# Attention norms, row broadcast and conv taps of the input projection moved to other ticks, and low parts of wide weights on one engine

## Chip, cores and metric

One Trainium2 chip, one core. The metric is the device time of one execution in microseconds; a median over runs is given.

## What is computed

One layer of a hybrid block on x of 1024 rows and 1024 columns, in float32 (depth 1):

```
h = rms_norm(x, mix_norm_g)
u = h @ w_in                       # 3328 columns, split over three mixers
q, k, v -> 4 heads of stick-breaking attention (q and k normed by head)
rq, rk, rv, rg -> 8 heads of retention in chunks, normed, times silu(rg)
a, gate -> GLU, causal depthwise conv of 31 taps, layer norm over 256 channels, silu
x = x + concat(three outputs) @ w_out
x = x + relu(rms_norm(x) @ w_ff1)^2 @ w_ff2
```

## The kernel before

**Products.** Every large product is done in three TensorE matmuls on float32 split in a high and a low part (`mm3`, L117): high by high, and the two mixed ones. For each weight chunk of 128 x 512 ScalarE copies the high part (L181, or L153 for chunks that go to a "wr" tile) and VectorE or GpSimd subtracts it to get the low part (L182, L154). Chunks come by DMA on SP's queue into five buffers, and a buffer is free for the next load when the low part is made.

**Input projection.** x is loaded with its norm's weights applied and multiplied at once by the first wide group (q and k of head pair 0, and v), L202 to L228, into all eight PSUM banks, which are then copied to SBUF (`raw0`). The row norm's factors `rstd` come at the end of that stage (`row_stats`, L243). After that the work is cut in ticks (`tick`, L269): in each, PE gets a part of a product, and before it the side work that was entered for that tick with `at_tick`, by its order number. Ticks 0 to 15: the narrow product for head pair 1 (`gemm_narrow`, 8 row tiles of 128, two ticks each, two PSUM banks "g"). Ticks 16 to 31: conv columns a and gate. Ticks 32 to 95: four wide groups of 16 ticks (`gemm_group`): k and v, then g and q of retention's first half, then the same for the second half. Ticks 96 to 111: the first half of the output projection (three of eight rows of w_out), then the rest, and the feed-forward part.

**Wide weights.** A wide group has eight chunks (`w_wide`, L141). Chunks are counted in `nwide` over all groups; 1 to 8 are the first group, 9 to 16 the second, 17 to 40 the third to fifth. An odd number has its low part on VectorE, an even one on GpSimd. Nine tiles hold them in turn, so of the eight chunks of a group all but one are split while the last row tile of the group before uses the same tiles.

**Side work.** `sb_norm` (L287) norms one row tile's q and k by head: a square on ScalarE, a sum on VectorE, a power on GpSimd (`rpow`), a product on VectorE. `sb_turn` (L301) transposes four tiles on PE and splits them. `sb_head` (L334) enters for each head 12 attention steps, one a tick: `a_step` (scores, sigmoids, scan, product), two ticks later `b_step` (transposes and split), then `c_step` (product by v). Tiles 0 to 3 of pair 0 are normed before tick 0, tiles 4 to 7 within `turn0(0)` at tick 1, and `turn0(1)` is at tick 3. `row_bcast` (L249), which spreads `rstd` over all partitions for the conv gate, is at tick 16. `qk1_evac` norms a tile of pair 1 two ticks after its product began, and frees its bank.

**Conv.** 124 taps (`conv_tap`, VectorE, L591), entered from tick 35 on by the list `per`; the late half of the rows (hf 1) first, then the early half. The layer norm of two row tiles has two parts, `conv_norm_a` and two ticks later `conv_norm_b` (L595, L616).

**Output projection.** `split_mixed` (L763) splits a 128-row part of the mixers' output; `out_proj` (L854) adds up three rows (0 to 2) for all output tiles first, then the other five (3 to 7) in the order of their numbers. The rows 6 and 7 are split after the last tick of side work.

The order on each engine's queue is not the code's order alone: when the program is built, a planner simulates the engines and takes the ready instruction that comes first in the code. Once built, each engine goes through its queue strictly in order.

Of the kernel before, what the change touches and what calls it, by code (L numbers as in the profile page):

```python
# [15 lines left out]
P = 128  # L16
# [3 lines left out]
NT = T // P  # L20
# [58 lines left out]
def build(tc, d):  # L79
# [59 lines left out]
    nwide = [0]  # L139

    def w_wide():  # L141

        c = wpos[1]
        wpos[1] += 1
        w_dma(c + RAW + (2 if c >= RAW else 0))
        n = nwide[0] % 9
        nwide[0] += 1
        lo_engine = V if nwide[0] % 2 else GP
        if n < WB:
            return w_split(raws[c], lo_engine)  # L150
        t = wp.tile([P, 1024], F32R, tag="wr", name=nm("ww"), bufs=3)
        hi, lo = t[:, 0:512], t[:, 512:1024]
        S.copy(hi, raws[c])  # L153
        lo_engine.tensor_tensor(out=lo, in0=raws[c], in1=hi.bitcast(F32), op=ALU.subtract)  # L154
        return hi, lo
# [93 lines left out]
    def row_bcast(out, col, tag, by="cv"):  # L249
        for hf in range(2):  # L250
            ps = bank(tag)
            dg = small(by, (P, 4, P))
# [34 lines left out]
    def sb_norm(pair, tt, src):  # L287
# [7 lines left out]
        if tt % 2 == 0:  # L295
            tb[tt // 2] = small("cv", (P, 2, 256))
        qn = tb[tt // 2][:, tt % 2, :]
# [3 lines left out]
    def sb_turn(pair, tg):  # L301
        pq, pk = bank("t"), bank("t")
        for u in range(4):
            qn = tb[2 * tg + u // 2][:, u % 2, :]
            TE.transpose(pq[:, u * P:u * P + P], qn[:, 0:P], ident)
            TE.transpose(pk[:, u * P:u * P + P], qn[:, P:2 * P], ident)
# [26 lines left out]

    def sb_head(pair, e, t0):  # L334
        h = 2 * pair + e
        tick0 = t0
        for m in range(4):
# [66 lines left out]
            for jg in range((2 * m + 1) // 4, -1, -1):  # L404
                for ii in range(2):
                    at_tick(t0, 30, lambda a=(m, jg, ii, None, st): a_step(*a))
                    at_tick(t0 + 2, 20, lambda a=(m, jg, ii, None, st): b_step(*a))
                    t0 += 1
                at_tick(t0 + 2, 10, lambda a=(m, jg, None, st): c_step(*a))
# [61 lines left out]
    def turn0(tg):  # L471
        sb_turn(0, tg)
        if tg == 0:
            norm0(range(4, 8))

    norm0(range(4))
    for tt in range(NT):
        v_evac(tt, raw0[tt // 2][:, tt % 2, 256:512])
    at_tick(1, 5, lambda: turn0(0))
    at_tick(3, 5, lambda: turn0(1))  # L480
    t1 = sb_head(0, 0, 2)
    t1 = sb_head(0, 1, t1)
    t1 = sb_head(1, 0, t1)
    sb_end = sb_head(1, 1, t1) + 4
# [9 lines left out]
    rbc = slot("DM")  # L494
    at_tick(now[0], 6, lambda: row_bcast(rbc, rstd, "o"))
# [137 lines left out]
    per = [1] * 22 + [2] * 7 + [3] * 16 + [2] * 20  # L633
# [4 lines left out]
    for t2, t in ((2, 81), (3, 85), (0, 100), (1, 102)):  # L638
# [215 lines left out]
    def out_proj(pi, dt, hf):  # L854
# [3 lines left out]
        for k in w:  # L858
            mm3(ps, w[k][0], w[k][1], mh[k][:, tsl], ml[k][:, tsl], k == min(w), k == max(w))
# [14 lines left out]
    for dt in range(NK):  # L874
        out_job(0, dt)
        if dt in (1, 5, 6):
            split_mixed({1: 3, 5: 4, 6: 5}[dt])
# [314 lines left out]
```

## Time and profile before

| | |
|---|---|
| median of 3 runs | 1157.6 us (1157.25 to 1157.94) |
| the profiled execution | 1159.54 us |
| its span, first to last instruction | 1157.8 us |
| mean granted TensorE clock | 0.992 |
| PE busy | 1121.4 us, 97% of the span |
| PE weight loads busy | 933.0 us, 81% |
| DVE busy | 897.7 us, 78% |
| ACT busy | 484.1 us, 42% |
| POOL busy | 519.1 us, 45% |

PE is TensorE, DVE VectorE, ACT ScalarE, POOL GpSimd, SP the DMA queue. A timeline row has its start, its duration, engine, code line, operation, output<-inputs, shapes and a count, and in brackets the idle time before it with the instruction that ended it. Matmuls overlap, so their durations are longer than the distance of their starts.

### The profile page before, as it was taken

To read this page: it belongs to the slowest core of one execution; us is meant where nothing else is said; L and a number is where in the kernel's file an instruction comes from. 1 tells how busy PE (TensorE), PEld (TensorE's weight loads), DVE (VectorE), ACT (ScalarE), POOL (GpSimd) and SP (SyncE) were. 2 spreads that over 40 slices of the span, in tenths; PEclk is the share of its full clock that TensorE was granted. 3 is DMA by queue.
4 is the path that set the end of the run, shared out by engine and by line. 5 is a ranking of instruction groups with operands and counts; after the bars stand their busy time and mean duration, and the time that the engine had idled before them with its cause. 6 is when DMAs were issued, how large, how long until landed. Compare 5 with 4: busy or idle time off the path is not lost.

```text
span 1157.8 us, 15678 instructions
## 1 busy us (share of the span) xinstructions
PE 1121.4 (97%) x5416; PEld 933.0 (81%) x5416; DVE 897.7 (78%) x1378; ACT 484.1 (42%) x917; POOL 519.1 (45%) x413
## 2 busy tenths in 40 slices
PE   8968899999999989999999999999999999999997
PEld 6857788888887878888888888888878788888886
DVE  7498677787899898579975666666699897886963
ACT  7366655453322242356433333333443443444441
POOL 4356234473555463242466565655583531522300
PEclk9989999999999989999999999999999999999999
DMA  8101011030202051112254444444787464552342
GB/s 277 48 1 46 19 42 55 19 110 15 87 24 87 20 217 61 55 73 91 78 187 148 152 161 140 164 146 141 279 304 264 130 219 129 164 182 82 110 136 73
DMA packets 63727, 137.00 MB, mean 118 GB/s; under 512 B 7200, under 2 KB 11936, under 8 KB 63648
## 3 DMA queue, kind: packets, MB, share of 16 engines
q1 hardware_dynamic: 63072, 135.56, 35.3%
q8 instruction: 43, 0.70, 0.3%
q10 hardware_dynamic: 576, 0.44, 0.1%
q14 instruction: 36, 0.29, 0.1%
HBM read 98.22 MB, written 37.75 MB: 117 GB/s over the span
## 4 chain that ended last, share of the span: by engine, by line
PE 47%; DVE 5%; issue 3%; POOL 2%; ACT 0%; DVEq 0%; POOLq 0%; ACTq 0%
PE g L119 4%; PE g L120 4%; PE g L118 4%; PE t L119 4%; PE t L118 4%; PE t L120 4%; PE o L119 4%; PE o L120 4%; PE o L118 4%; PE z L119 4%; PE z L118 4%; PE z L120 4%; DVE wlo L182 1%; POOL sum L903 1%; POOL wr L903 0%
## 5 line engine op out<-in xcount | busy, mean ns | idle before, releaser
L182 DVE TENSOR_TENSOR wlo<-sum,whi 128x512 fp32r<-128x512 f32 x78 | 80.2, 1029 | 84.2 <-ACT whi L181 84.1
L181 ACT CAST whi<-sum 128x512 fp32r<-128x512 f32 x78 | 47.9, 617 | 101.4 <-POOL sum L903 50.9
L182 DVE TENSOR_TENSOR wlo<-wr,whi 128x512 fp32r<-128x512 f32 x80 | 76.4, 960 | 6.9 <-ACT whi L181 6.9
L908 POOL TENSOR_TENSOR sum<-wr 128x512 f32<-128x512 f32 x16 | 23.4, 1466 | 120.2 <-DMA wr<-in_w_ff_dram 92.7
L365 POOL TENSOR_TENSOR be<-be,kp 128x512 f32<-128x512 f32 (+3 forms) x48 | 44.6, 932 | 70.5 <-DVE kp L361 33.1
L181 ACT CAST whi<-wr 128x512 fp32r<-128x512 f32 x80 | 48.2, 620 | 51.7 <-PE t L119 17.6
L196 POOL TENSOR_TENSOR rs<-ss,nhalf 128x4 f32<-128x4 f32 (+1 forms) x36 | 36.8, 1024 | 66.8 <-DVE ss L699 44.7
L361 DVE TENSOR_TENSOR_SCAN kp<-kp 128x512 f32<-128x512 f32 (+3 forms) x48 | 53.4, 1118 | 10.1 <-ACT kp L354 9.8
L591 DVE SCALAR_TENSOR_TENSOR DM__439_2052<-glu,vec,DM__439_2052 128x512 f32<-128x512 f32 x60 | 52.7, 921 | 0.0
L591 DVE SCALAR_TENSOR_TENSOR glu<-glu,vec 128x512 f32<-128x512 f32 x60 | 50.3, 881 | 0.0
L354 ACT ACTIVATE kp<-z 128x512 f32<-128x512 f32 (+3 forms) x48 | 23.7, 493 | 36.2 <-PE z L351 22.0
L182 POOL TENSOR_TENSOR wlo<-wraw,whi 128x512 fp32r<-128x512 f32 x18 | 28.4, 1585 | 22.6 <-ACT whi L181 21.2
L903 POOL TENSOR_TENSOR sum<-wr,sum 128x512 f32<-128x512 f32 x19 | 32.8, 1725 | 9.9 <-DVE wlo L182 9.9
L903 POOL TENSOR_TENSOR sum<-sum,wr 128x512 f32<-128x512 f32 x18 | 24.4, 1357 | 12.5 <-DVE wlo L182 12.5
L376 PE MATMUL t<-ident,be 128*128 128x128 f32 x144 | 25.1, 276 | 4.2 <-DVE P__108_534 L315 1.6
L181 ACT CAST whi<-wraw 128x512 fp32r<-128x512 f32 x33 | 20.1, 619 | 19.5 <-PE g L119 10.0
L563 POOL TENSOR_TENSOR P__538_2584<-P__397_1882 128x128 f32<-128x128 f32 x16 | 14.5, 906 | 29.0 <-DVE P__397_1882 L561 29.0
L182 POOL TENSOR_TENSOR wlo<-rawq,whi 128x512 fp32r<-128x512 f32 x14 | 23.7, 1699 | 7.8 <-ACT whi L181 7.5
L355 ACT ACTIVATE be<-z 128x512 f32<-128x512 f32 (+3 forms) x48 | 23.7, 493 | 8.4 <-PE t L376 8.4
L376 PEld LDWEIGHTS t<-ident,be 128*128 128x128 f32 x144 | 16.9, 140 | 8.1 <-issue 5.7
L903 POOL TENSOR_TENSOR wr<-wr,wr 128x512 f32<-128x512 f32 x16 | 22.5, 1406 | 1.1
L681 ACT ACTIVATE e<-o 128x256 f32<-128x256 f32 x16 | 6.2, 385 | 38.6 <-PE o L679 37.9
(2941 smaller groups left out, 4141.6 us busy)
## 6 DMA issues: line engine op xcount, KB each, us to landing
wr<-in_w_ff_dram SPq DMA_DIRECT2D x40, 512.0 KB, 3.9
wraw<-in_w_in_dram SPq DMA_DIRECT2D x32, 256.0 KB, 2.7
rawq<-in_w_in_dram SPq DMA_DIRECT2D x20, 256.0 KB, 2.8
P__396_1881<-in_rot_dram SPq DMA_DIRECT2D x32, 128.0 KB, 2.0
wraw<-in_w_out_dram SPq DMA_DIRECT2D x10, 256.0 KB, 2.8
rawq<-in_w_out_dram SPq DMA_DIRECT2D x6, 256.0 KB, 3.5
P__18_144<-in_xT_dram SPq DMA_DIRECT2D x1, 512.0 KB, 5.1
P__24_182<-in_xT_dram SPq DMA_DIRECT2D x1, 512.0 KB, 6.2
```

Source lines behind the costliest of these rows:

```text
L118: TE.matmul(out, lh, rh, start=start, stop=False, skip_group_check=on)
L119: TE.matmul(out, lh, rl, start=False, stop=False, skip_group_check=on)
L120: TE.matmul(out, ll, rh, start=False, stop=stop, skip_group_check=on)
L181: S.copy(hi, raw)
L182: (lo_engine or GP).tensor_tensor(out=lo, in0=raw, in1=hi.bitcast(F32), op=ALU.subtract)
L196: GP.tensor_tensor(out=out, in0=in_, in1=nhalf[:, 0:in_.shape[1]], op=ALU.pow)
L354: S.activation(kp[:, 0:n], pz[:, 0:n], AF.Sigmoid, scale=-0.125)
L361: V.tensor_tensor_scan(rev, rev, rev, kp[:, n:n + 1], op0=ALU.mult, op1=ALU.bypass)
L365: GP.tensor_tensor(out=be[:, 0:n], in0=be[:, 0:n], in1=kp[:, 1:n + 1], op=ALU.mult)
L376: TE.transpose(pt[:, j * P:j * P + P], be[:, j * P:j * P + P], ident)
L591: V.scalar_tensor_tensor(out=acc, in0=src, scalar=vec[:, o:o + 1], in1=acc, op0=ALU.mult, op1=ALU.add)
L903: (eng or GP).tensor_tensor(out=o, in0=x, in1=y, op=ALU.subtract)
```

## The change

The low parts of wide chunks from number 17 on are all made on POOL. `row_bcast` is done before tick 0, with its operands in two pages instead of the "cv" buffers. All eight tiles of pair 0 are normed before tick 0, into pages of their own; their two turns are at ticks 3 and 6 instead of 1 and 3. Attention steps follow a list of ticks: ten from tick 6 on, one a tick; then 20 in ticks 16 to 30; then one a tick from 31. The taps from tick 35: one a tick for 15 ticks, two for 14, three for 16, then one and two in turn for 16, then one for 9, up to tick 104. The layer norms begin at ticks 72, 76, 105 and 107 (81, 85, 100 and 102 before). The second half of the output projection adds up the rows in the order 3, 6, 7, 4, 5, and rows 4 and 5 are both split after output tile 6 of the first half.

```diff
--- before.py
+++ after.py
@@ -145,7 +145,7 @@
         w_dma(c + RAW + (2 if c >= RAW else 0))
         n = nwide[0] % 9
         nwide[0] += 1
-        lo_engine = V if nwide[0] % 2 else GP
+        lo_engine = V if nwide[0] % 2 and nwide[0] <= 16 else GP
         if n < WB:
             return w_split(raws[c], lo_engine)
         t = wp.tile([P, 1024], F32R, tag="wr", name=nm("ww"), bufs=3)
@@ -249,7 +249,7 @@
     def row_bcast(out, col, tag, by="cv"):
         for hf in range(2):
             ps = bank(tag)
-            dg = small(by, (P, 4, P))
+            dg = small(by, (P, 4, P)) if by else page(10 + hf, (P, 4, P))
             V.tensor_tensor(out=dg, in0=ident.unsqueeze(1).to_broadcast([P, 4, P]),
                             in1=col[:, 4 * hf:4 * hf + 4].unsqueeze(2).to_broadcast([P, 4, P]), op=ALU.mult)
             TE.matmul(ps, ones, dg.rearrange("p a b -> p (a b)"), start=True, stop=True)
@@ -293,15 +293,18 @@
         rs = small("rs", (P, 4))
         rpow(rs, ss)
         if tt % 2 == 0:
-            tb[tt // 2] = small("cv", (P, 2, 256))
-        qn = tb[tt // 2][:, tt % 2, :]
+            if pair == 0:
+                tb[0, tt // 2] = nrm0[tt // 4][:, tt % 4:tt % 4 + 2, :]
+            else:
+                tb[1, tt // 2] = small("cv", (P, 2, 256))
+        qn = tb[pair, tt // 2][:, tt % 2, :]
         V.tensor_tensor(out=qn.rearrange("p (a b) -> p a b", b=DH), in0=src.rearrange("p (a b) -> p a b", b=DH),
                         in1=rs.unsqueeze(2).to_broadcast([P, 4, DH]), op=ALU.mult)
 
     def sb_turn(pair, tg):
         pq, pk = bank("t"), bank("t")
         for u in range(4):
-            qn = tb[2 * tg + u // 2][:, u % 2, :]
+            qn = tb[pair, 2 * tg + u // 2][:, u % 2, :]
             TE.transpose(pq[:, u * P:u * P + P], qn[:, 0:P], ident)
             TE.transpose(pk[:, u * P:u * P + P], qn[:, P:2 * P], ident)
         ts = slice(tg * 512, tg * 512 + 512)
@@ -331,9 +334,11 @@
 
     mix_sb = {}
 
+
+    sb_ticks = list(range(6, 16)) + [16 + 3 * (i // 4) + (0, 0, 1, 2)[i % 4] for i in range(20)] + list(range(31, 60))
+
     def sb_head(pair, e, t0):
         h = 2 * pair + e
-        tick0 = t0
         for m in range(4):
             st = {"carry": {}, "first": True}
 
@@ -403,10 +408,10 @@
 
             for jg in range((2 * m + 1) // 4, -1, -1):
                 for ii in range(2):
-                    at_tick(t0, 30, lambda a=(m, jg, ii, None, st): a_step(*a))
-                    at_tick(t0 + 2, 20, lambda a=(m, jg, ii, None, st): b_step(*a))
+                    at_tick(sb_ticks[t0], 30, lambda a=(m, jg, ii, None, st): a_step(*a))
+                    at_tick(sb_ticks[t0] + 2, 20, lambda a=(m, jg, ii, None, st): b_step(*a))
                     t0 += 1
-                at_tick(t0 + 2, 10, lambda a=(m, jg, None, st): c_step(*a))
+                at_tick(sb_ticks[t0] + 2, 10, lambda a=(m, jg, None, st): c_step(*a))
         return t0
 
     def parts(n, lo_engine=None):
@@ -470,18 +475,19 @@
 
     def turn0(tg):
         sb_turn(0, tg)
-        if tg == 0:
-            norm0(range(4, 8))
-
-    norm0(range(4))
+
+    rbc = slot("DM")
+    row_bcast(rbc, rstd, "o", None)
+    nrm0 = [page(19, (P, 4, 256)), page(10, (P, 4, 256))]
+    norm0(range(NT))
     for tt in range(NT):
         v_evac(tt, raw0[tt // 2][:, tt % 2, 256:512])
-    at_tick(1, 5, lambda: turn0(0))
-    at_tick(3, 5, lambda: turn0(1))
-    t1 = sb_head(0, 0, 2)
+    at_tick(3, 5, lambda: turn0(0))
+    at_tick(6, 5, lambda: turn0(1))
+    t1 = sb_head(0, 0, 0)
     t1 = sb_head(0, 1, t1)
     t1 = sb_head(1, 0, t1)
-    sb_end = sb_head(1, 1, t1) + 4
+    sb_head(1, 1, t1)
     mix_sb[1] = page(17)
     sb_prepare(1)
 
@@ -491,8 +497,6 @@
             at_tick(now[0] + 1, 5, lambda: sb_turn(1, tt // 4))
 
     gemm_narrow(qk1_evac)
-    rbc = slot("DM")
-    at_tick(now[0], 6, lambda: row_bcast(rbc, rstd, "o"))
     glu = [None, None]
 
     def conv_gate(ct, hf, pa, pgt):
@@ -630,12 +634,12 @@
 
     c0 = 35
     taps = [(ct, hf, j) for hf in (1, 0) for j in range(TAPS) for ct in range(2)]
-    per = [1] * 22 + [2] * 7 + [3] * 16 + [2] * 20
+    per = [1] * 15 + [2] * 14 + [3] * 16 + [1, 2] * 8 + [1] * 9
     n, t = 0, c0
     while n < len(taps):
         at_tick(t, 40, lambda a=taps[n:n + per[t - c0]]: conv_taps(a))
         n, t = n + per[t - c0], t + 1
-    for t2, t in ((2, 81), (3, 85), (0, 100), (1, 102)):
+    for t2, t in ((2, 72), (3, 76), (0, 105), (1, 107)):
         at_tick(t, 25, lambda t2=t2: conv_norm_a(t2))
         at_tick(t + 2, 25, lambda t2=t2: conv_norm_b(t2))
 
@@ -855,8 +859,9 @@
         tsl = slice(512 * hf, 512 * hf + 512)
         w = taken[pi, dt]
         ps = bank("o" if pi else "g")
-        for k in w:
-            mm3(ps, w[k][0], w[k][1], mh[k][:, tsl], ml[k][:, tsl], k == min(w), k == max(w))
+        ks = (3, 6, 7, 4, 5) if pi else tuple(w)
+        for k in ks:
+            mm3(ps, w[k][0], w[k][1], mh[k][:, tsl], ml[k][:, tsl], k == ks[0], k == ks[-1])
         V.tensor_tensor(out=x2[dt][:, tsl], in0=ps, in1=x2[dt][:, tsl], op=ALU.add)
 
     jobs = [(pi, dt) for pi in range(2) for dt in range(NK)]
@@ -873,8 +878,11 @@
 
     for dt in range(NK):
         out_job(0, dt)
-        if dt in (1, 5, 6):
-            split_mixed({1: 3, 5: 4, 6: 5}[dt])
+        if dt == 1:
+            split_mixed(3)
+        if dt == 6:
+            split_mixed(4)
+            split_mixed(5)
     while steps:
         tick()
     for hf in range(2):
```

## Rows read from the trace of the kernel before

**Rows 1.** Windows: stretch, length, busy us of PE PEld DVE ACT POOL, PEclk, DMA, GB/s

```profile
50.00:130.00 80.00, 64.46 (x424) 55.64 (x424) 64.88 (x142) 49.99 (x107) 39.10 (x38) 0.94 0.06 17
...
300.00:390.00 90.00, 87.33 (x446) 72.80 (x445) 87.89 (x145) 24.37 (x56) 48.47 (x46) 1.00 0.21 67
390.00:400.00 10.00, 10.00 (x74) 9.29 (x73) 5.60 (x17) 3.41 (x9) 3.86 (x5) 1.00 0.00 1
...
420.00:430.00 10.00, 6.86 (x42) 5.98 (x42) 9.95 (x16) 4.41 (x11) 6.32 (x5) 0.92 0.97 366
430.00:440.00 10.00, 9.34 (x35) 7.45 (x35) 9.95 (x22) 0.75 (x2) 5.99 (x7) 0.74 0.68 263
440.00:490.00 50.00, 49.78 (x267) 41.97 (x266) 35.19 (x74) 16.68 (x37) 11.83 (x14) 1.00 0.15 45
```

**Rows 2.** Timeline of PE, 54 to 105 us: narrow product, attention, first conv matmul

```profile
54.92 0.28 PE L118 MATMUL g<-whi,xh__12_101 128*128 128x256 f32 x1
...
57.68 0.29 PE L120 MATMUL g<-whi,xl__59_380 128*128 128x256 f32 x1
...
72.23 0.41 PE L118 MATMUL g<-whi,xh__12_101 128*128 128x256 f32 x1
...
102.47 0.62 PE L376 MATMUL t<-ident,be 128*128 128x128 f32 x4
...
103.16 0.39 PE L351 MATMUL z<-P__70_448,P__69_447 128*128 128x512 f32 x1
...
104.79 0.50 PE L118 MATMUL g<-xh__12_101,whi 128*128 128x512 f32 x1 [1.11 <-DVE cv L298]
```

**Rows 3.** Timeline of DVE, 63 to 72 us: turn, scans, first evacuation

```profile
63.61 0.74 DVE L315 SCALAR_TENSOR_TENSOR P__69_447<-t,vec,P__69_447 64x512 fp32r<-64x512 f32 x1
...
70.29 1.13 DVE L361 TENSOR_TENSOR_SCAN kp<-kp 128x128 f32<-128x128 f32 x2
71.45 0.42 DVE L298 TENSOR_TENSOR cv<-g,rs 128x256 f32<-128x256 f32 x1
```

**Rows 4.** Timeline of PE at 428 us: retention's output waits for its state

```profile
428.26 0.76 PE L678 MATMUL o<-P__396_1881,P__538_2584 128*128 128x128 f32 x2 [3.13 <-DVE P__396_1881 L695]
```

**Rows 5.** Timeline of DVE and PE, 124 to 127 us: the row broadcast

```profile
124.13 0.72 DVE L253 TENSOR_TENSOR cv<-ident,rstd 128x512 f32<-128x512 f32 x1
...
124.91 1.12 PE L255 MATMUL o<-cv,ones 128*128 128x512 f32 x2 [0.59 <-DVE cv L253]
126.50 1.10 PE L255 MATMUL o<-cv,ones 128*128 128x512 f32 x2 [0.47 <-DVE kp L357]
```

**Rows 6.** Taps of line L591 (ns min/median/max); timeline of DVE and POOL at 304

```profile
L591 DVE SCALAR_TENSOR_TENSOR glu<-glu,vec x60: 710/742/1778, 343.2 to 443.8; 128x512 f32<-128x512 f32 x60
...
304.15 1.76 DVE L591 SCALAR_TENSOR_TENSOR DM__439_2052<-glu,vec,DM__439_2052 128x512 f32<-128x512 f32 x1
...
303.64 1.72 POOL L182 TENSOR_TENSOR wlo<-rawq,whi 128x512 fp32r<-128x512 f32 x1
```

**Rows 7.** Timeline of POOL and PE at the boundaries of the last three wide groups

```profile
235.44 1.94 POOL L154 TENSOR_TENSOR ww<-rawq,ww 128x512 fp32r<-128x512 f32 x1
...
243.99 1.74 POOL L182 TENSOR_TENSOR wlo<-wraw,whi 128x512 fp32r<-128x512 f32 x1
...
247.80 0.39 PE L118 MATMUL g<-whi,xh__58_379 128*128 128x512 f32 x1
...
307.22 1.71 POOL L182 TENSOR_TENSOR wlo<-wraw,whi 128x512 fp32r<-128x512 f32 x1 [1.86 <-ACT whi L181]
309.32 1.32 POOL L196 TENSOR_TENSOR rs<-ss,nhalf 128x4 f32<-128x4 f32 x1 [0.40 <-DVE ss L699]
310.63 1.27 POOL L182 TENSOR_TENSOR wlo<-rawq,whi 128x512 fp32r<-128x512 f32 x1
...
315.27 0.39 PE L118 MATMUL g<-whi,xh__58_379 128*128 128x512 f32 x1
...
365.74 1.27 POOL L182 TENSOR_TENSOR wlo<-wraw,whi 128x512 fp32r<-128x512 f32 x1 [2.26 <-ACT whi L181]
```

## Prediction, made before the changed kernel ran

> **What bounds the kernel now.** I read the windows first, because the page's slices are too coarse for waits of one to three microseconds. TensorE (PE) is the bound: from 130 us on it is nearly always busy. So the time is PE's work, plus its idle time, plus what is lost while its clock is granted at half. Two places hold nearly all that this change can reach [rows 1]. From 50 to 130 us PE is busy 64.46 of 80 us, so 15.5 us are idle, with VectorE (DVE) busy 64.88; the mean granted clock of 0.94 stands for 0.06 x 80 x 2 = 9.6 us at 1.2 GHz, of which PE worked some 6.6 us, so that about 3.3 us are lost. From 420 to 440 us PE idles 3.1 + 0.7 us, and 0.92 and 0.74 stand for 1.6 + 5.2 = 6.8 us at half clock, 3.4 us lost. Between them, from 300 to 390 us, DVE is saturated (87.89 of 90) while PE loses only 2.7 us.
>
> Then I read the two places in order of time. In the first, the last matmul of the narrow product's first two row tiles stands at 57.68 and the next one of that product at 72.23 [rows 2]. What it needs is a PSUM bank: both banks "g" are full until the first evacuation ends, and that evacuation's last DVE operation starts only at 71.45 [rows 3], because it stands in DVE's queue behind the head-pair-0 turn, of which 63.61 is the first row, and two scans at 70.29. In the second place the planner has put splits of the mixed rows ahead of retention's state update, DVE comes late to it, and PE waits 3.13 us at 428.26 [rows 4].
>
> **Part A: norms, row broadcast and turn moved at the start.** All PE work here stays; it is only placed elsewhere. The two products of the DVE row broadcast (0.72 and, alike, 0.7 us, [rows 5]) come ahead of the gate at 71.45: +1.4 us. The pair-0 turn now has tick 3 and stands behind the first evacuation (tick 2): two L315, two L318 and two L321, with 0.74 for the first [rows 3]; the six sum to 3.8 us. The scans of 1.13 us [rows 3] go to tick 6. So the gate opens at 72.23 + 1.4 - 3.8 - 1.1 = 68.7, 3.5 us earlier. What this buys is less than 3.5, since PE had used the wait for transposes and for four score steps, which now follow. From the gate to the first conv matmul at 104.79 lie 12 ticks of 1.44 us (24 matmuls from 54.92 to 57.80 are two ticks, [rows 2]) = 17.3 us; the other 15.3 us are side work and waits, and I leave them but for 0.9 us that the steps kept from the wait add. The conv product then starts 2.6 us earlier. It begins with about two more attention steps still to do: four transposes are 0.62 us and a score product 0.39 [rows 2], with the products by the values about 1.4 us a step by estimate, so +2.8 us. The row broadcast's two PE products (1.12 and 1.10) are gone from there, -2.2, and with them their waits of 0.59 and 0.47 [rows 5], -1.1. **A = -2.6 + 2.8 - 2.2 - 1.1 = -3.1 us.** The broadcast's products now lie in idle time and cost nothing; if that cover is gone they are +2.2. One wait is new: the norms of tiles 4 to 7 go into the page from which PE reads the broadcast's first product, so they, and on DVE all queued behind them, the first evacuation too, wait for PE to have read it. PE does this before DVE comes to tile 4, so 0; else one product, +1.1. The ends: +1.4 if the evacuation is planned no earlier and the broadcast only delays it; -10 if DVE, with 15.1 us unused in the 80 [rows 1], is kept busy there. I take a value near the small end, as PE is not the engine that sets this stage.
>
> The attention steps that are moved into the conv product's ticks put 20 steps into 15 ticks. DVE has room there, and PE is full anyway, so they cost what they cost before.
>
> **Part B: fewer taps late.** Ticks 80 to 95 hold 24 taps instead of 32; eight go to ticks 50 to 63 or to 96 and after, where DVE has room (35.19 of 50 us from 440 to 490, [rows 1]). Only the last half counts: from 390 to 400 DVE is idle for 4.4 us [rows 1], so no delay is carried over it. Ticks 88 to 95 lose four taps of 0.742 us [rows 6], 3.0 us, against the 3.13 us by which the state update came late [rows 4]. With it PE's wait goes to about 0.1, and the clock has no reason to fall: 3.1 + 3.4 = 6.5 us. The planner may put the splits, or other things, there again. **B = -4.5 us**, with ends 0 and -7.2 (also the 0.66 us that remain of the idle time).
>
> **Part C: the early half of the conv norm**, moved from ticks 81 and 85 to 72 and 76, and the taps of ticks 80 to 87. PE loses 2.7 us from 300 to 390; I take **-0.5 us**, with ends 0 and -2.7.
>
> **Part D: low parts on POOL alone.** Of the 24 wide chunks from the third group on, 12 low parts leave DVE. It hardly helps DVE: beside a POOL low part of 1.72 us a tap takes 1.76 instead of 0.742 [rows 6], so each moved operation takes about 1.0 us from DVE and gives back a like time. What counts is when POOL has the last low part of a group. At the first boundary POOL has no gap from 235.44 to the end of the last low part at 243.99 + 1.74 = 245.7; three more of 1.7 put that at 250.9, and PE wants it at 248.0 (its high part goes in at 247.80): 2.9 us late [rows 7]. Behind them on POOL wait the attention's products and the rotary; the transposes and the retention wait for those. The loaded chunk is freed later too, and with it the next load on SP, by no more than the low part is late. At the second boundary POOL waits 1.86 us for the high part, the last low part ends at 311.9, and three more of 1.5 to 1.7 less that gap make 315.1 at most, against 315.27. At the third it has 2.26 us of waiting [rows 7] and is taken at 0. So ends of 0 and +2.9; PE can put side work into the wait, and I take **D = +1.5 us**.
>
> **Part E: the end of the conv chain.** The last norm goes from tick 104 to 109 and the splits of rows 4 and 5 follow it; against that the second half of the output projection takes 3, 6, 7 before 4, 5. From 440 to 490 PE idles only 0.22 us [rows 1]. Two norms of five ticks later have the whole last job as cover; **+0.5 us**, with ends 0 and +2.
>
> DMA sources, sizes and their queue (SP) stay in the same order; POOL issues none. The sum: -3.1 - 4.5 - 0.5 + 1.5 + 0.5 = **-6.1 us**. The profiled execution took 1159.54 us, 1.7 over its span and 1.9 over the median 1157.6; the sum makes it 1153.4, and a median of **1151.5 us**.
>
> **The rivals.** (1) POOL becomes the bound at the boundaries, and the change is slower. For: POOL is gapless at the first one, and its low parts stretch when DVE works beside them (1.72 and 1.74 against 1.27, 1.94 at most in these rows, [rows 6, 7]). Against: at the other two it has waiting time left. At 2.2 us each the first boundary comes out 2.9 + 6 x 0.5 = 5.9 us late, the second 303.64 + 6 x 2.2 + 1.32 (a norm's power between them, [rows 7]) = 318.2 against 315.27, 2.9 late, and the third like it: 11.7 in all, -8.1 + 11.7 + 0.5 = +4.1, 1161.7 us. It decides from 7.6 us of waits in all, a mean of about 2.0 us a low part. The Trainium skill (SBUF — State Buffer, Who interferes with whom) says that VectorE with two SBUF operands and GpSimd exclude each other on a shared port pair, the later one standing still for the whole instruction. The stretched tap and low part agree with it; by that rule this rival's time would be the one to expect if each low part met a whole DVE operation. (2) Only one half of the gain comes: the planner again queues splits ahead of the state update, so B = 0: -1.6 us, 1156.0. The order on each queue is planned at compile time, which speaks for it; the shorter DVE queue speaks against. A case of this is that the moves do not move anything, as PE already ran four ticks ahead of the turn: A = 0 and B = -4.5 give 1154.6. (3) More is gained: A near -8, B near -6.5: 1144.6. DVE's unused 15.1 us speak for it; the chain DVE, POOL, DVE of each norm speaks against.
>
> **How the numbers follow.** Forecast 0.50, rival 1 0.13, rival 2 0.22, rival 3 0.15. About 0.2% (2.3 us) is what a measurement of this kernel can tell from no change. The forecast and rival 3 are faster by more, with a small part of rival 2 (1154.6): 0.67; the rest of rival 2 and a small part of the rest are within it: 0.20; slower 0.13. The range takes the forecast, most of rival 3 and rival 2: 1144.5 to 1158.5.
>
> **What would show it.** A: the gap from 57.68 to the fifth tick shrinks to some 11 us and the conv product starts near 102; wrong if the first evacuation still stands behind the turn. B: no wait of 3 us and no clock below 1 around 415 to 435. D: low parts of POOL in a row at each boundary, and PE waits on them under 3 us in all; wrong if they hold PE longer than 7 us. E: no PE wait over 2 us at the first jobs of the second half.

## The result, and the profile after

| | before | changed |
|---|---|---|
| median | 1157.77 us (1157.25 to 1159.38, 4 runs) | 1169.26 us (1166.27 to 1170.57, 4 runs) |
| ratio | | 1.0093, 95% interval 1.007 to 1.0116 |
| profiled execution, its span | 1159.54, 1157.8 us | 1170.57, 1168.8 us |
| mean granted clock | 0.992 | 0.985 |

The change costs about 1%, where 6 us less were forecast. The page of the changed kernel, its first lines and the slices of PE and of its clock:

```profile
span 1168.8 us, 15654 instructions
...
PE 1128.3 (97%) x5416; PEld 938.5 (80%) x5416; DVE 886.8 (76%) x1366; ACT 482.4 (41%) x917; POOL 540.7 (46%) x425
...
PE   8969999999999898999999999999999999999998
...
PEclk9979999999999999999999999999999999999999
```

PE has as many matmuls as before; at the lower mean clock they take 7 us longer, and PE idles 4 us more. DVE has 11 us less to do and POOL 22 more, but neither sum says where the time went. The windows do (columns as in [rows 1]):

```profile
50.00:130.00 80.00, 67.91 (x414) 58.99 (x413) 59.49 (x132) 45.27 (x93) 35.72 (x33) 0.89 0.06 17
...
360.00:370.00 10.00, 7.51 (x33) 5.04 (x33) 10.00 (x12) 4.63 (x10) 10.00 (x8) 1.00 0.35 93
370.00:380.00 10.00, 9.48 (x38) 7.49 (x36) 5.72 (x13) 1.26 (x3) 7.56 (x8) 0.83 0.49 144
380.00:390.00 10.00, 7.22 (x26) 5.62 (x27) 8.27 (x14) 2.12 (x5) 5.21 (x6) 0.83 0.09 28
430.00:440.00 10.00, 7.72 (x48) 6.21 (x46) 10.00 (x10) 7.14 (x17) 9.04 (x7) 1.00 1.00 374
440.00:450.00 10.00, 7.61 (x39) 7.05 (x40) 9.94 (x22) 0.38 (x1) 3.33 (x4) 0.83 0.81 315
...
490.00:500.00 10.00, 6.67 (x25) 4.93 (x24) 4.84 (x7) 2.98 (x5) 1.46 (x2) 0.84 0.01 2
```

Three places behind 300 us are new or no better: the third group boundary (360 to 390), where before PE lost only 2.7 us in 90 [rows 1]; the place where PE waited for retention's state update (430 to 450), as bad as before; and 490 to 500, where before there was hardly a wait. The timeline of PE there and at the start of the conv product, each with the wait ahead of it in brackets:

```profile
100.88 0.50 PE L118 MATMUL g<-xh__12_101,whi 128*128 128x512 f32 x1 [0.57 <-DVE cv L301]
...
366.14 0.50 PE L119 MATMUL g<-ww,xh__31_222 128*128 128x512 f32 x1 [0.72 <-POOL ww L154]
367.83 0.50 PE L119 MATMUL g<-wlo,xh__40_265 128*128 128x512 f32 x1 [0.72 <-POOL wlo L182]
...
381.91 0.41 PE L660 MATMUL t<-ident,P__398_1903 128*128 128x128 f32 x2 [2.43 <-DVE e L632]
...
442.39 0.98 PE L671 MATMUL z<-P__543_2611,P__544_2612 128*128 128x128 f32 x3 [3.91 <-DVE P__545_2613 L672]
...
496.08 0.73 PE L118 MATMUL o<-xh__875_4690,whi 128*128 128x512 f32 x2 [2.85 <-ACT xh__875_4690 L773]
```

The first line answers to 104.79 in [rows 2]: the conv product starts 3.9 us earlier, as part A wanted. The wait of 3.91 answers to the 3.13 of [rows 4]; PE now waits there for another retention operation on DVE, the masking of the scores (L672), where before it waited for the state.

To see where time is won or lost I set the two traces side by side by the PE work that is still to do, and took the difference of the times: the **offset**, negative where a kernel is ahead of the kernel before. For the changed kernel it is -2.9 us at 240 us, 0 at 340, +8.9 at 395, +7.5 at 480, +12.6 at 505 and some +13 at the end (its span is only 11 longer, since the stretch behind the last matmul is 2 us shorter). Where the order of PE's work differs, how the matmuls are weighed moves such a value by about 1 us. So the start wins some 3 us, the boundaries up to 340 lose 3, the third boundary with the conv norm 9, and the tail 5.

One trace's offset is not sharp. The kernel e2 below has the same PE queue as the kernel before up to some 180 us, and still its offset is +4.3 at 140 us, some 3 of them gathered between 80 and 140. Its windows show why: the granted clock is 0.83 in two slices where that of before is 1.00:

```profile
80.00:90.00 10.00, 8.59 (x55) 8.18 (x56) 7.06 (x20) 4.38 (x12) 4.76 (x6) 0.83 0.01 2
...
130.00:140.00 10.00, 8.17 (x32) 6.34 (x31) 5.54 (x12) 3.42 (x7) 0.41 (x1) 0.83 0.00 0
```

So I read rises within a stretch, and medians for the sums.

### The profile page after: what moved, and what is told of

It reads as the page before. It is cut to its first block, busy times and chain, and to the rows that moved or that the text cites. A ratio compares the mean times of both kernels' runs of the same rounds, so it can differ in the third digit from the quotient of the medians.

```text
span 1168.8 us, 15654 instructions
## 1 busy us (share of the span) xinstructions
PE 1128.3 (97%) x5416; PEld 938.5 (80%) x5416; DVE 886.8 (76%) x1366; ACT 482.4 (41%) x917; POOL 540.7 (46%) x425
## 4 chain that ended last, share of the span: by engine, by line
PE 81%; DVE 11%; issue 2%; POOL 2%; DMA 2%; ACT 1%; SPq 0%; POOLq 0%; DVEq 0%; ACTq 0%
PE g L118 11%; PE g L119 10%; PE g L120 10%; PE t L118 5%; PE t L119 5%; PE t L120 5%; PE o L119 5%; PE o L120 5%; PE o L118 5%; PE z L119 4%; PE z L118 4%; PE z L120 4%; DVE DM__444_2079 L595 2%; DVE glu L595 2%; PE o L400 1%
## 5 line engine op out<-in xcount | busy, mean ns | idle before, releaser
L182 DVE TENSOR_TENSOR wlo<-sum,whi 128x512 fp32r<-128x512 f32 x78 | 83.1, 1066 | 79.5 <-ACT whi L181 79.4
L595 DVE SCALAR_TENSOR_TENSOR glu<-glu,vec 128x512 f32<-128x512 f32 x60 | 53.0, 925 | 0.1
L182 POOL TENSOR_TENSOR wlo<-wraw,whi 128x512 fp32r<-128x512 f32 x23 | 36.3, 1590 | 16.9 <-ACT whi L181 16.9
L182 POOL TENSOR_TENSOR wlo<-rawq,whi 128x512 fp32r<-128x512 f32 x17 | 27.8, 1642 | 21.2 <-ACT whi L181 21.2
L911 POOL TENSOR_TENSOR sum<-sum,wr 128x512 f32<-128x512 f32 x18 | 25.3, 1405 | 12.6 <-DVE wlo L182 12.6
L567 POOL TENSOR_TENSOR P__543_2611<-P__403_1908 128x128 f32<-128x128 f32 x16 | 14.7, 918 | 28.5 <-DVE P__403_1908 L565 19.7
L671 PE MATMUL z<-P__543_2611,P__544_2612 128*128 128x128 f32 x128 | 18.6, 287 | 3.9 <-DVE P__545_2613 L672 3.9
L181 ACT CAST whi<-rawq 128x512 fp32r<-128x512 f32 x23 | 14.0, 618 | 18.4 <-issue 12.8
```

The source lines that it names most:

```text
L181: S.copy(hi, raw)
L182: (lo_engine or GP).tensor_tensor(out=lo, in0=raw, in1=hi.bitcast(F32), op=ALU.subtract)
L595: V.scalar_tensor_tensor(out=acc, in0=src, scalar=vec[:, o:o + 1], in1=acc, op0=ALU.mult, op1=ALU.add)
L911: (eng or GP).tensor_tensor(out=o, in0=x, in1=y, op=ALU.subtract)
```

## The experiments

| kernel | median us (runs) | ratio to before, 95% interval |
|---|---|---|
| e1_moves_only | 1167.52 (4) | 1.0057 to 1.0098 |
| e2_lo_only | 1162.49 (9) | 1.0020 to 1.0044 |
| e3_norm_later | 1160.94 (10) | 1.0005 to 1.0038 |
| e4_last_group_split | 1164.68 (4) | 1.0039 to 1.0073 |
| e5_start_only | 1154.66 (9) | 0.9943 to 0.9976 |
| e6_tail_as_before | 1162.29 (11) | 1.0015 to 1.0044 |
| e7_start_and_taps | 1155.35 (12) | 0.9968 to 1.0000 |
| e8_norm_early_only | 1167.66 (7) | 1.0045 to 1.0089 |
| e9_split_on_pool | 1156.26 (11) | 0.9967 to 0.9988 |
| e10_no_late_taps | 1151.91 (4) | 0.9935 to 0.9963 |
| e11_one_norm_early | 1158.88 (11) | 0.9989 to 1.0014 |
| e12_norm_early_fewer_taps | 1154.56 (10) | 0.9960 to 0.9981 |
| e13_start_norm_taps | 1152.01 (6) | 0.9920 to 0.9959 |
| e14_change_taps_moved | 1155.54 (12) | 0.9960 to 0.9990 |
| e15_taps_off_both | 1152.12 (7) | 0.9929 to 0.9964 |

The kernel before had medians of 1158.19 (e1 to e4), 1158.31 (e5 to e8), 1158.55 (e9 to e12) and 1158.40 (e13 to e15) beside them. "Over before" is against these.

### Which part costs: undoing one at a time (e1 to e4)

e1, against the changed kernel:

```diff
-        lo_engine = V if nwide[0] % 2 and nwide[0] <= 16 else GP
+        lo_engine = V if nwide[0] % 2 else GP
```

> All the moves of the change, but low parts of wide chunks in turn on VectorE and GpSimd as before. Theory P (the loss is GpSimd's queue at the last two group boundaries: behind the low parts there stand the conv norm's power and products, and TensorE waits): most of the 12 us come back that TensorE is late by at the end, and the time is at or below that of the kernel before, 1148 to 1157 us. Theory N (the early half of the conv norm, moved onto the boundary, and the late end of the conv chain cost it, whoever makes the low parts): 1163 to 1169 us, and TensorE still loses over 6 us from 355 to 395 us.

e2 makes the opposite edit in the kernel before.

> The kernel before with nothing but the low parts from chunk 17 on made by GpSimd. Theory P: slower than the kernel before by 3 to 9 us (1161 to 1167), with TensorE's waits at the wide groups' boundaries. Theory N: within 3 us of the kernel before (1155 to 1161), as no conv norm lies at a boundary.

e3 and e4, each against the changed kernel:

```diff
-    for t2, t in ((2, 72), (3, 76), (0, 105), (1, 107)):
+    for t2, t in ((2, 81), (3, 85), (0, 105), (1, 107)):
```

> The changed kernel with the first two conv norms back at ticks 81 and 85 (72 and 76 in the change). Theory N: the 8.6 us that TensorE loses from 355 to 395 us fall to under 3, 1161 to 1164 us. Theory P: the low parts of the last boundary still hold TensorE and the norm, 1167 to 1171 us.

```diff
-        lo_engine = V if nwide[0] % 2 and nwide[0] <= 16 else GP
+        lo_engine = V if nwide[0] % 2 and not 16 < nwide[0] <= 32 else GP
```

> The changed kernel, but in the last wide group alone (chunks 33 to 40) the odd low parts are made by VectorE again; the queues differ from the changed kernel only around that boundary. Theory P: of the 8.6 us lost from 355 to 395 us at least 5 come back, 1160 to 1165 us. Theory N: under 2 us come back, 1167 to 1170 us.

The changed kernel is 11.5 us over before. Without POOL's low parts (e1) it is still 9.3 over; with the first two conv norms back (e3) only 2.8; the low parts alone (e2) cost 4.3. So the early norm is a large term; the low parts cost less, and within the change (e1 against it) less than the two intervals can separate. e1 shows that the norm does not need them: at the third boundary its offset rises from +1.5 to +9.6, with PE waiting 2.17 and 1.53 us for low parts of DVE in place of POOL's. In e4 the time is one that theory P names, but the place is not: the rise from 360 to 400 us is 6.9 against 8.6 in the changed kernel, and the rest of its 5 us lies ahead of that place, where the clock's chance shifts are as large, so e4 tells little of the last group. In all of e1, e3 and e4 PE waits 2.85 or 2.86 us between 487 and 497 us for ACT's split of the late conv row, and the offset rises by 4 to 6 there.

### The third boundary (e8, e11, e12)

e8, against the kernel before (its taps end their late half in tick 72, so 73 is the first tick that can take a norm):

```diff
-    for t2, t in ((2, 81), (3, 85), (0, 100), (1, 102)):
+    for t2, t in ((2, 73), (3, 77), (0, 100), (1, 102)):
```

> The kernel before with only the first two conv norms moved from ticks 81 and 85 to 73 and 77 (the taps as before end their first half at 72). Theory N (the norm's chain over PE, DVE, POOL and ACT at the third group boundary costs PE by itself): the offset rises by 5 to 8 us from 350 to 400 us, waits of over 1.5 us on PE at the norm's transposes or at the retention behind them, 1163 to 1166 us. Theory P (it costs only together with low parts that POOL makes alone): under 2 us, 1158 to 1160 us.

1167.66: these eight ticks alone cost 9.4 us, nearly as much as the whole change. Theory N holds, and POOL's rule is not needed. Windows of e8, then its timeline at the boundary:

```profile
340.00:350.00 10.00, 10.00 (x49) 8.16 (x48) 10.00 (x18) 1.58 (x4) 3.78 (x4) 1.00 0.08 26
350.00:360.00 10.00, 10.00 (x50) 8.36 (x49) 10.00 (x19) 2.77 (x6) 4.27 (x5) 1.00 0.09 27
...
370.00:380.00 10.00, 8.63 (x28) 6.65 (x28) 7.39 (x14) 0.47 (x1) 4.78 (x5) 0.68 0.36 108
```

```profile
367.11 1.21 DVE L182 TENSOR_TENSOR wlo<-rawq,whi 128x512 fp32r<-128x512 f32 x1
...
370.09 1.59 DVE L182 TENSOR_TENSOR wlo<-wraw,whi 128x512 fp32r<-128x512 f32 x1
...
381.92 0.54 DVE L628 TENSOR_SCALAR e<-t,vec 128x256 f32<-128x256 f32 x1 [4.54 <-ACT e L626]
...
368.37 0.50 PE L119 MATMUL g<-wlo,xh__40_265 128*128 128x512 f32 x1 [2.17 <-DVE wlo L182]
371.74 0.80 PE L119 MATMUL g<-wlo,xh__52_341 128*128 128x512 f32 x1 [1.36 <-DVE wlo L182]
383.85 0.41 PE L656 MATMUL t<-ident,P__392_1877 128*128 128x128 f32 x2 [2.43 <-DVE e L628]
```

DVE has no gap from 340 us to the boundary. The norm's operations come on top, and so both low parts that PE needs there start late. PE waits for them, its clock falls to half (0.68 in the slice), and the transposes of the second norm come late on PE. DVE then stands 4.54 us for the sigmoid behind these, and PE 2.43 us for a "t" bank that this norm still holds: the delay goes round from one engine to the next.

e11, against the kernel before:

```diff
-    for t2, t in ((2, 81), (3, 85), (0, 100), (1, 102)):
+    for t2, t in ((2, 73), (3, 85), (0, 100), (1, 102)):
```

> The kernel before with only the first conv norm moved, from tick 81 to 73; the second stays at 85. Theory 1 (the loss of the early norms comes from the second one, whose products now stand at the third group boundary): under 2 us, 1158 to 1160 us, no PE wait of 2.43 us near 384 us. Theory 2 (each norm costs by its own work that DVE has to do before the boundary): half the loss, 1162 to 1163 us. Theory 3 (the first one carries it): 1165 us or more.

1158.88, 0.3 over before: theory 1 in time. Some waits came at the boundary (2.82 for a low part of DVE at 370.16) and were made good later. So the loss comes with the second norm. That norm moved alone was not run, so the loss may also need both.

e12 is e8 with fewer taps in ticks 73 to 80. By the list `per` they are 8 instead of 23, fifteen fewer, and not eight as the expectation below says; from tick 81 on it has three a tick, 24 in ticks 88 to 95 where before has 16:

```diff
-    per = [1] * 22 + [2] * 7 + [3] * 16 + [2] * 20
+    per = [1] * 22 + [2] * 7 + [3] * 9 + [1] * 8 + [3] * 18
```

> The kernel with the early norms alone (ticks 73 and 77), and eight taps fewer in ticks 73 to 80: one a tick there, three a tick behind them. Theory 1 (DVE is overfull ahead of the boundary, so low parts and the norm come late): the waits of 2.17 and 1.36 us on DVE's low parts go, and the offset against the kernel before rises by under 4 us instead of 8 from 350 to 400 us, 1161 to 1163 us. Theory 2 (the norm's chain over four engines with two banks and queues in fixed order makes the waits, whatever DVE's load): the 2.43 us at the transposes of the retention stay and the rise is 6 us or more, 1166 us.

1154.56: 13.1 us under e8 by moving 15 x 0.742 = 11.1 us of DVE work [rows 6] behind the boundary, and 4.0 under before. (In the traces 12 of L591's taps start from 340 to 370 us, in e8 23.) Theory 1, and more than it asked. The relief without the early norms was not run, so the 4.0 may be the relief's alone, and what the norms cost on a relieved DVE is not shown. Windows of e12, then its low parts:

```profile
340.00:350.00 10.00, 10.00 (x48) 8.16 (x48) 7.97 (x18) 1.58 (x4) 4.48 (x5) 1.00 0.09 26
350.00:360.00 10.00, 10.00 (x50) 8.32 (x49) 7.49 (x17) 3.95 (x8) 5.37 (x7) 1.00 0.10 28
360.00:370.00 10.00, 10.00 (x49) 8.27 (x48) 10.00 (x12) 3.62 (x7) 10.00 (x8) 1.00 0.57 170
```

```profile
361.58 1.22 DVE L182 TENSOR_TENSOR wlo<-rawq,whi 128x512 fp32r<-128x512 f32 x1
...
366.13 1.00 DVE L182 TENSOR_TENSOR wlo<-wraw,whi 128x512 fp32r<-128x512 f32 x1
```

DVE has 4.5 us to spare in the 20 ahead of the boundary, the low parts start 5.5 and 4.0 us earlier, and PE works through 360 to 370 without a gap.

### The tail (e6)

e6, against the changed kernel:

```diff
-    per = [1] * 15 + [2] * 14 + [3] * 16 + [1, 2] * 8 + [1] * 9
-    for t2, t in ((2, 72), (3, 76), (0, 105), (1, 107)):
+    per = [1] * 15 + [2] * 14 + [3] * 16 + [2] * 20
+    for t2, t in ((2, 72), (3, 76), (0, 100), (1, 102)):
-        ks = (3, 6, 7, 4, 5) if pi else tuple(w)
+        ks = tuple(w)
-        if dt == 1:
-            split_mixed(3)
-        if dt == 6:
-            split_mixed(4)
-            split_mixed(5)
+        if dt in (1, 5, 6):
+            split_mixed({1: 3, 5: 4, 6: 5}[dt])
```

> The changed kernel with part E undone: conv norms of the rows 0 and 1 at ticks 100 and 102, no tap after tick 96, the splits of rows 3, 4 and 5 after jobs 1, 5 and 6, the rows of the second half in rising order. Theory 1 (the wait of 2.85 us for the split of row 4 and the half clock behind it belong to part E): no wait of over 1 us on PE from 480 to 505 us, the offset rises there by under 1 us instead of 5, 1164.5 us. Theory 2 (the wait there comes from PE's place against ACT, POOL and DVE after the stall at 440, whatever the tail's order): it stays, or one of like size takes its place, 1168 to 1170 us.

1162.29, 7.5 us less against its own before. The offset is 7.3 at 480 us and 6.2 at 505, so theory 1 holds. The edit also puts the taps of ticks 80 to 95 back to two a tick (part B); PE's wait there is 4.52 us at 441.53, no better than 3.91, so the gain does not come from them. Its window in the tail:

```profile
490.00:500.00 10.00, 10.00 (x46) 8.29 (x45) 3.28 (x5) 3.95 (x6) 0.00 (x0) 1.00 0.34 105
```

In the changed kernel the last norm's transposes stand on PE's queue right ahead of the products that need their result. Timeline of PE, DVE, POOL and ACT:

```profile
492.64 0.60 PE L625 MATMUL t<-ident,cv 128*128 128x128 f32 x4
...
494.04 0.54 DVE L632 TENSOR_SCALAR e<-t,vec 128x256 f32<-128x256 f32 x1
...
495.27 0.54 DVE L632 TENSOR_SCALAR e<-t,vec 128x256 f32<-128x256 f32 x1 [0.69 <-ACT e L630]
...
494.66 0.72 POOL L633 TENSOR_TENSOR glu<-e,e 128x256 f32<-128x256 f32 x1 [6.08 <-DVE e L632]
...
495.41 0.62 ACT L773 CAST xh__875_4690<-glu 128x512 fp32r<-128x512 f32 x1 [0.18 <-POOL glu L633]
```

PE has nothing between them, so transpose, sigmoid, scale, product and split lie open, 2.85 us, and then PE works at half clock (1.2 instead of 2.4 GHz; 0.84 in the slice).

### The start, and the state update (e5, e7, e9, e10)

e5 is part A alone. Against the changed kernel it has the tail's order of e6 and

```diff
-        lo_engine = V if nwide[0] % 2 and nwide[0] <= 16 else GP
+        lo_engine = V if nwide[0] % 2 else GP
-    per = [1] * 15 + [2] * 14 + [3] * 16 + [1, 2] * 8 + [1] * 9
-    for t2, t in ((2, 72), (3, 76), (0, 105), (1, 107)):
+    per = [1] * 22 + [2] * 7 + [3] * 16 + [2] * 20
+    for t2, t in ((2, 81), (3, 85), (0, 100), (1, 102)):
```

> The kernel before with part A alone: norms of tiles 4 to 7, row broadcast, turns and attention steps moved at the start; low parts, taps, conv norms and output projection as before. Theory 1 (the parts add up, and part A keeps its size): the offset of PE's progress is about -4 us from 140 to 340 us and stays there, 1154 us. Theory 2 (what is gained at the start is given back where DVE is saturated, 300 to 390 us, since PE there is no more the engine that sets the pace): -4 at 240 us, 0 to -1 at 390 us, 1157.5 us.

1154.66, 3.7 us under before. The offset is -5.7 at 240 us and still -4.0 at 390: theory 1. Over all traces, the eleven kernels with part A have a mean offset of -4.7 at 240 us and the five without it +1.6. Window of e5 from 50 to 130 us, then its timeline: first and last operation of the turn on DVE, the first evacuation, the gate and the conv product:

```profile
50.00:130.00 80.00, 67.78 (x431) 59.12 (x429) 60.29 (x134) 47.75 (x98) 38.07 (x37) 0.94 0.06 17
```

```profile
65.12 0.74 DVE L318 SCALAR_TENSOR_TENSOR P__69_447<-t,vec,P__69_447 64x512 fp32r<-64x512 f32 x1
...
71.22 0.42 DVE L324 CAST P__73_451<-P__74_452 64x512 fp32r<-64x512 f32 x1
...
72.94 0.42 DVE L301 TENSOR_TENSOR cv<-g,rs 128x256 f32<-128x256 f32 x1
...
73.55 0.46 PE L118 MATMUL g<-whi,xh__12_101 128*128 128x256 f32 x1
...
99.32 0.50 PE L118 MATMUL g<-xh__12_101,whi 128*128 128x512 f32 x1 [0.57 <-DVE cv L301]
```

e7, against e5:

```diff
-    per = [1] * 22 + [2] * 7 + [3] * 16 + [2] * 20
+    per = [1] * 15 + [2] * 14 + [3] * 16 + [2] * 20
```

> The kernel before with part A and eight taps moved from ticks 35 to 57 and from the end to ticks 50 to 63, so that the last tap comes four ticks sooner; low parts, norms and the tail as before. If the state update's wait near 430 us comes from the taps in DVE's queue, as the prediction had it, the wait is under 1 us there and the time is 3 to 6 us under that of the start alone, 1148 to 1151 us. If it comes from the order of the splits and the retention on DVE, the wait stays at 3 us or more and the time is within 1.5 us of the start alone.

1155.35, 0.7 over e5; waits of 2.07 and 2.25 us stay at 425 and 433. That is the second reading in time, but the edit could not show the first: by the list it moves seven taps ahead and ends three ticks sooner, and it leaves two taps a tick in ticks 80 to 95 as before. So e7 says nothing about fewer taps there; e10, e13 and e15 do. Its offset also shows a loss of about 4 us at 320 to 340, behind a wait of 1.84 for POOL.

e9 is e5 with two of the seven low parts of the mixed rows on POOL:

```diff
-            V.tensor_tensor(out=ml[k][:, cs], in0=src, in1=mh[k][:, cs].bitcast(F32), op=ALU.subtract)
+            eng = GP if hf == 1 and k in (1, 2) else V
+            eng.tensor_tensor(out=ml[k][:, cs], in0=src, in1=mh[k][:, cs].bitcast(F32), op=ALU.subtract)
```

> The start alone (part A), and two of the seven low parts of the mixed rows that stand in a row on DVE near 425 us (second half of the rows 1 and 2) made by POOL. Theory 1 (the wait for the state update is the length of that burst on DVE, stretched by POOL's low parts beside it): the waits of 2.06 and 3.89 us at 423 and 431 us shrink to under 1.5 us in all and the clock stays up, 1149 to 1151 us. Theory 2 (the output projection then waits for POOL instead): a PE wait of 2 us or more on POOL, 1154 us or more.

1156.26, and PE waits 2.72 and 2.80 us at 423.79 and 432.30, both for DVE: neither theory. Its time does not differ from e5's beyond the two intervals. Work given to POOL does not relieve DVE here: the five of the seven splits that are left on DVE take 8.15 us in e9, and all seven take 8.37 in e5. Timeline of DVE in e9, the last two of them:

```profile
419.29 3.44 DVE L775 TENSOR_TENSOR xl__825_4463<-P__548_2619,xh__824_4462 128x512 fp32r<-128x512 f32 x2
```

The timeline of the changed kernel shows the same (DVE, then POOL):

```profile
435.91 3.46 DVE L774 TENSOR_TENSOR xl__793_4300<-P__547_2618,xh__792_4299 128x512 fp32r<-128x512 f32 x2
439.29 2.34 DVE L774 TENSOR_TENSOR xl__825_4458<-P__548_2619,xh__824_4457 128x512 fp32r<-128x512 f32 x2
441.56 0.68 DVE L672 TENSOR_TENSOR P__545_2613<-z,P__546_2616 128x512 f32<-128x512 f32 x1
...
433.71 1.73 POOL L182 TENSOR_TENSOR wlo<-rawq,whi 128x512 fp32r<-128x512 f32 x1
435.39 5.10 POOL L182 TENSOR_TENSOR wlo<-wraw,whi 128x512 fp32r<-128x512 f32 x3
```

Splits beside POOL's low parts take 1.73 us each, alone 0.67 (at 442.16 us). The masking of the scores that PE waits for (441.56) is queued behind them. The Trainium skill (SBUF — State Buffer, Who interferes with whom) says that a VectorE instruction with two SBUF inputs contends with a GpSimd instruction that reads SBUF; the rows agree.

e10, against the kernel before:

```diff
-        at_tick(t, 40, lambda a=taps[n:n + per[t - c0]]: conv_taps(a))
+        if not 88 <= t < 96:
+            at_tick(t, 40, lambda a=taps[n:n + per[t - c0]]: conv_taps(a))
```

> The kernel before with the 16 taps of ticks 88 to 95 left out (11.9 us of DVE time at 0.742 each). If taps that DVE has to do first make the state update late, as part B of the prediction had it, the wait of 3.13 us at 428 us is gone (under 0.5) and the time is 6 us less, 1152 us. If the burst of splits by itself makes the wait, 2 us or more of it stay there and the time is within 2 us of before.

1151.91, 6.6 under before. The wait of 3.13 is gone, and the offset goes from +2.1 at 425 us to -4.3 at 430: 6.4 us, which is what the prediction had for the place (3.1 + 3.4). DVE comes to the splits with time in hand, ahead of POOL's row of low parts (from 429.03 here), and they are short, 0.80 us each, with the masking of the scores behind them (timeline of DVE):

```profile
427.18 1.60 DVE L771 TENSOR_TENSOR xl__827_4449<-P__543_2592,xh__826_4448 128x512 fp32r<-128x512 f32 x2
...
429.43 0.68 DVE L669 TENSOR_TENSOR P__540_2586<-z,P__541_2589 128x512 f32<-128x512 f32 x1
```

### Do the gains add up (e13 to e15)

e13 is e5 with the edits of e8 and e12; e14 is e13 with the low-part rule of the changed kernel (the lines of e1, the other way round).

> Part A, and the first two conv norms at ticks 73 and 77 with one tap a tick in 73 to 80; low parts and the tail as before. Theory 1 (gains at different places add up: about -4 at the start, about -4 from the relieved boundary): 1150 to 1151 us. Theory 2 (every new set lets the planner order the queues anew, and a gain of one place is lost at another): 1154 to 1157 us.

1152.01, 6.4 under before, and the gains of e5 and e12 would add up to 7.6. That is 1 us outside theory 1's range and 2 outside theory 2's, so nearer to theory 1. This version is faster than both kernels (0.9920 to 0.9959 of before) with the norm early and the start moved. With 24 taps in ticks 88 to 95 its wait at the state update is the longest of all; timeline of PE:

```profile
429.42 0.80 PE L682 MATMUL o<-P__402_1907,P__543_2611 128*128 128x128 f32 x2 [6.54 <-DVE P__402_1907 L699]
```

> The same with the low parts from the third wide group on made by POOL alone. Theory 1 (POOL's low parts cost only where DVE is overfull): within 1.5 us of the kernel without that rule. Theory 2 (they cost by themselves at the three boundaries, as the rule alone cost the kernel before 4 us): 3 to 5 us more, with PE waits on POOL's low parts near 250, 315 and 365 us.

1155.54, 3.5 over e13, and the intervals of the two do not overlap: theory 2 by the medians. But PE's waits on POOL at the boundaries stay under 1 us. From 240 to 360 us e14 loses 1.6 us more than e13, and from 415 to 445 some 3 us more, where PE waits 2.20 and 5.80 us in e14 and 6.54 in e13. The trace of e14 also starts 2 us worse, with a granted clock of 0.83 from 80 to 90 and from 120 to 130 us where e13 has 1.00, and it is an execution of 1158.44 us, 2.9 over its median; so it does not say which of these losses the median has.

e15, against e13:

```diff
-    per = [1] * 22 + [2] * 7 + [3] * 9 + [1] * 8 + [3] * 18
-    for t2, t in ((2, 73), (3, 77), (0, 100), (1, 102)):
+    per = [1] * 22 + [2] * 7 + [3] * 9 + [1] * 8 + [4] * 7 + [1] * 8 + [3] * 6
+    for t2, t in ((2, 73), (3, 77), (0, 102), (1, 104)):
```

> Part A and the early norms, with one tap a tick both in 73 to 80 and in 88 to 95, four a tick between and three behind, last two norms at 102 and 104. If the state update's wait is set by the taps queued ahead of it, the PE wait of 3 us or more between 420 and 445 us falls under 1 us and the time is 3 to 5 us under the kernel with the first relief alone, 1146 to 1148 us. If the burst of splits sets it, the wait stays.

1152.12, no better than e13, and neither reading in full: PE waits 3.60 at 426.70, yet the offset goes from -5.0 at 415 us to -8.5 at 445, so with 8 taps in ticks 88 to 95 the place costs 3.5 us less than in the kernel before with 16 (2 to 4 by how the matmuls are weighed). The tail takes it back, from -9.1 at 475 to -4.0 at 485, with two ticks of delay of the last norms. Timeline of PE in e15:

```profile
477.38 0.73 PE L118 MATMUL o<-xh__873_4668,whi 128*128 128x512 f32 x2 [2.75 <-ACT xh__873_4668 L773]
```

## Why the prediction was wrong, point by point

The forecast was 1151.5 us with a range of 1144.5 to 1158.5; 1169.26 lies outside, on the other side of before.

**What bounds the kernel** was right: PE, its idle time and its clock.

**Part A: right in size by luck, wrong in its route.** -3.1 was forecast and e5 gave -3.7. But the gate did not open at 68.7: the first evacuation still stands behind the norms, the whole turn (65.12 to 71.64 in e5) and the scans (72.94), and the gate is at 73.55, later than 72.23 [rows 2]. The 3.8 and 1.1 us that were to leave the queue ahead of it did not, as the case under rival 2 had it. The gain lies behind the gate. From there to the conv product are 25.8 us instead of 32.6, where I had held the 15.3 us of side work and waits fixed. In this stretch e5 has 24 matmuls of attention instead of 57, as the new list of ticks puts steps behind the conv product's start, and PE waits 2.9 us instead of 5.1. From 50 to 130 us PE idles 12.2 us in e5 and 15.5 before [rows 1], at the same mean clock of 0.94: that is 3.3 of the 3.7 us.

**Part C: this step failed most.** It put -0.5 us with ends 0 and -2.7, since PE loses only 2.7 us from 300 to 390. That is a bound of what can be won, and I used it as the bound of the effect. The same row says that DVE is busy 87.89 of the 90 [rows 1], so what is moved ahead there pushes something PE needs. Alone the move costs 9.4 us (e8), and 8.7 in the changed kernel (e3 against it). With fifteen taps taken out of ticks 73 to 80 the loss is gone (e12): the room for the move was not made.

**Part D: mis-sized.** +1.5, with ends 0 and +2.9; measured 4.3 alone (e2), 3.5 on a relieved DVE (e14 against e13) and 2.2 within the change (e1 against it, where the intervals overlap). That each low part on POOL takes back from DVE about what it gives is right only where the two stand side by side. By the pages of three pairs DVE is relieved over the whole execution: its busy time falls by 8.1 us from before to e2 (897.7 to 889.6), by 9.0 from e13 to e14 and by 10.1 from e1 to the changed kernel, and POOL's rises by 16 to 18. So the time rose although DVE had less to do. Side by side, four taps take 6.42 us in the changed kernel instead of 3.0, and the norm's power waits behind POOL's low parts (timeline at the third boundary, DVE, then POOL):

```profile
361.91 6.42 DVE L595 SCALAR_TENSOR_TENSOR glu<-glu,vec 128x512 f32<-128x512 f32 x4
...
376.88 1.00 DVE L616 TENSOR_SCALAR cv<-t,bmv,rs 128x256 f32<-128x256 f32 x2 [2.15 <-POOL rs L196]
...
372.51 2.97 POOL L182 TENSOR_TENSOR wlo<-wraw,whi 128x512 fp32r<-128x512 f32 x2
...
376.14 0.71 POOL L196 TENSOR_TENSOR rs<-ss,nhalf 128x2 f32<-128x2 f32 x1
```

I had looked for the price in PE's waits on POOL, which are 0.72 us each, and not in what else is queued on POOL. The third boundary, "taken at 0", may be where the step failed; e4, which was to show it, is not sharp enough.

**Part E: mis-sized.** +0.5 with ends 0 and +2 stood on "the whole last job as cover". The products of rows 3, 6 and 7 ran earlier, and the transposes stood right ahead of the products of row 4. The wait is 2.85 us, the offset rises by 5.1, and undoing it gives 7.5 (e6). e6 undoes the norms' ticks, the splits and the order of the rows together, so which of them made the wait is read from PE's queue and not shown by a run.

**Part B: right mechanism, too little moved.** The wait was to fall from 3.13 to 0.1 by four taps less; it is 3.91. With 16 taps less it is gone, for the 6.4 us of my upper working (e10); eight taps less win about half of it (e15), and with eight more the wait is 6.54 (e13). What I left out is that the splits ahead of the update stretch from 0.67 to 1.73 us when they meet POOL's low parts, so that a small lead of DVE is used up; this last is read from the timelines and no run tests it by itself.

**The rivals.** Rival 2's B = 0 describes part B, and its case of the turn the gate of part A. Rival 1 had the sign, but not the cause: without its low parts the moves still cost 9.3 us (e1), and POOL's low parts took 1.59 and 1.64 us on average in the two rows of the changed kernel's page, not 2.0 or more. What was missing is a rival for part C, DVE as the bound ahead of the third boundary; it stood in the very row from which I took the small price.

The single prices, -3.7 + 8.7 + 2.2 + 7.5 = 14.7, exceed the measured 11.5 by 3 us. Each is a difference of medians with an interval of some 2 us to either side, so whether the parts overlap is not shown. What of POOL's low parts costs time in e2 and e14 stays open: behind 180 us, where its queue first differs, the trace of e2 loses only some 2 of the 4.3 us.

## What to carry to other kernels

The idle time of the bounding engine in a stretch, with the clock lost behind it, bounds what a move can win there, not what it can lose; for the loss read how full the engine is that takes the moved work, and what is queued behind it. Before side work goes earlier into a full stretch, take as much out of it: fifteen taps decided between +9.4 and -4.0 us. A chain over four engines, as that of the last norm here, needs other work on the bounding engine's own queue between its last input and its first use, and that is seen in the order of that queue, not in the length of the job around it.

## What the runs showed of the hardware

Waits of 1.4 to 2.9 us on PE were followed by stretches at half clock (0.68 at 370 to 380 us in e8, 0.84 at 490 to 500 in the changed kernel), so that the wait of 2.85 us cost 5.1. But not every such wait was: behind 2.06 us at 423.10 in e5 and 2.25 at 433.58 in e7 the slice's granted clock stayed at 1.00. With an identical queue the clock also fell in one execution and not in another (e2 at 80 and 130 us), which moved one trace by some 3 us.

VectorE operations that read PSUM were not stretched beside POOL's low parts: in the changed kernel L563, which reads a PSUM tile, took 0.47 us at 368.25 while POOL made a low part, as in all its 32 executions (0.46 to 0.48), and the taps around it, all from SBUF, 1.6 on average.
